# Side work beside a matmul stream: steps weighted by their work, none beside the rotations, and three shared PSUM banks instead of two and one

## The chip, the cores and the metric

The kernel runs on one core of one Trainium2 chip. TensorE (PE) multiplies matrices and writes its products to PSUM; VectorE (DVE) and ScalarE (ACT) read them from there. Each engine works through its own list of instructions in order and waits, where it must, on semaphores. The metric is the device time of one execution in microseconds (us).

## The reference, cut to what matters

One block with two branches on the same normalized input h (512 positions by 2048 channels), both cut from one wide projection:

```
h = rmsnorm(x, g_norm) * (1 + scl) + shift
r_q, r_k, r_v, r_g, n_q, n_kc, ..., m_a, m_b = split(h @ w_in)
y_ret = retention(rope(r_q), rope(r_k), r_v) * silu(r_g)      # 8 heads, chunks of 128
y_nsa = nsa_attention(rope(n_q), ...) * silu(n_g)             # 8 query heads, 2 kv groups
merged = sigmoid(m_a) * (y_ret @ w_up_ret) + sigmoid(m_b) * (y_nsa @ w_up_nsa)
out = rmsnorm(x + gate * (merged @ w_out), g_final)
```

`nsa_attention` is the part that the change schedules: each query attends to compressed keys, to selected blocks and to a window; with 512 positions the last two are causal softmax attentions over all earlier keys, each with its own keys and values. The three outputs are added with gates.

## The kernel before, in words

The projections are the main stream. A weight item of 128x1024 is loaded by SP into one of five raw buffers, ACT rounds it to `whi` (line 267), DVE writes the rest to `wlo` (line 268), and three matmuls (high by high, high by low, low by high) stand for one fp32 product (line 420). A `Group` is one block of 512 output columns: 8 items, 192 matmuls, four accumulators (tiles `g5_0` to `g5_3`) in four large banks. The groups that matter here, in order: g4 (`nq1`), g5 (`rq0`), g6 (`rk0`), g7 (`rv0`), g8 (`rg0`), g9 (`rq1`), g10 (`rk1`), g11 (`rv1`), g12 (`rg1`), g13 and g14 (`ng0`, `ng1`), then eight gate groups.

`Group.block` issues the work of one item as four steps, one accumulator (6 matmuls) each; its first act is to split the weights two items ahead. The last block of a group has two items, so 12 matmuls a step, and each of its steps ends with the evacuation of its accumulator (`self.ev`). For nq, rq and rk this is `rope`: two copies on ACT (lines 496 and 497), three passes on DVE (lines 498 to 500), through one `rot` buffer, so that one rotation follows the other.

After each step `tick` adds `rate` times the items of the step to a credit, and takes steps off the queue `side` while there is credit of 1 (line 383). From g5 on the queue holds `nsa_units`: 16 quads (four heads of one kv group, one 128-row block i of queries, one of the two softmax branches), each with four `scores` (one fp32 matmul of 128*(i+1) columns; mask and minimum on DVE, line 679; exponential on ACT, line 681; reciprocal and scaling on DVE, lines 682 and 683), `turn`s (four transposes into one bank, then a cast on ACT, line 731, and a subtraction on DVE, line 732) and `av`s (three matmuls, line 744). `c_scores`, `c_turn` and `c_av` do the compressed branch. When they are done, `ret_units` (retention) follow at a rate of 0.2; the last part of a head, `r3`, is a chain of some twenty small DVE instructions. What is left of `side` after mb3 is run at once.

PSUM has eight banks: four for groups, one for `o`, two for score tiles (`sbank`) and one for transposed tiles (`tbank`). A tile's bank comes free when the last engine has read the tile.

Tile names in what follows: `sc103` is the score tile of quad 10, head 3; `tp100` the transposes of quad 10, key block 0; `tp30c` those of the compressed branch.

Of the kernel before, what the change touches and what calls it, by code (L numbers as in the profile page):

```python
# [22 lines left out]
NK = D // P  # L23
# [62 lines left out]
def block_kernel(ctx: ExitStack, tc: tile.TileContext, t_in, out):  # L86
# [12 lines left out]
    def bank(tag, bufs, name):  # L99
        return ps.tile([P, 512], F32, tag=tag, bufs=bufs, name=name)  # L100
# [2 lines left out]
        return bank("pg", 4, name)  # L103

    def sbank(name):
        return bank("pss", 2, name)

    def tbank(name):
        return bank("pst", 1, name)

    def obank(name):
        return bank("pso", 1, name)
# [263 lines left out]


    side = deque()
    credit = [0.0]
    RATE_N, RATE_R = 0.72, 0.2  # L380
    rate = [0.0]

    def tick(w=1):
        credit[0] = min(credit[0] + rate[0] * w, 2.0)
        while credit[0] >= 1.0 and side:
            side.popleft()()
            credit[0] -= 1.0

    def flush():
        while side:  # L390
# [2 lines left out]
    class Group:  # L393


        def __init__(self, kind, banks, a_hi, a_lo, nk, ev, k0=0):
            self.kind, self.banks, self.a_hi, self.a_lo, self.nk, self.ev = kind, banks, a_hi, a_lo, nk, ev
            self.kk, self.k0 = 0, k0

        def steps(self, items):  # L400

# [27 lines left out]
        def block(self, items):  # L429
            load(items[0])  # L430
            n0 = w_ord[items[0]]
            split(max(n0 + 2, n0 + len(items) - 1))
            for st in self.steps(items):
                st()
                tick(len(items))

    def run_group(grp, idx, n, between=None, tail=2):

# [18 lines left out]
    hhi = lambda kk: h_hi[kk // 8][:, kk % 8, :]  # L457
    hlo = lambda kk: h_lo[kk // 8][:, kk % 8, :]
# [201 lines left out]
    def nsa_units():  # L660


        quads = [(i, g, br) for i in range(NT) for g in range(2) for br in range(2)]
# [3 lines left out]
        def scores(q, r):  # L667
            i, g, br = quads[q]
            if "pq" not in res:
                res["pq"] = bigt("pq")  # L670
            b = sbank(f"sc{q}{r}")
            n = P * (i + 1)
            h = 4 * g + r
            nc.tensor.matmul(b[:, :n], res["qT"][:, h, i * P:(i + 1) * P], res["kT"][:, 2 * br + g, :n],  # L674
                             start=True, stop=True)
            p = res["pq"][:, count[0] % 8, :]
            count[0] += 1
            sm = wk.tile([P, 3], F32, tag="sm", bufs=3, name=f"sm{q}{r}")
            nc.vector.tensor_tensor_reduce(p[:, :n], b[:, :n], mask[:, 512 - n:], -SCALE, 3.0e38,  # L679
                                           OP.add, OP.min, sm[:, 0:1])  # L680
            nc.scalar.activation(p[:, :n], p[:, :n], AF.Exp, bias=sm[:, 0:1], scale=-1.0, accum_out=sm[:, 1:2])  # L681
            nc.vector.reciprocal(sm[:, 2:3], sm[:, 1:2])
            nc.vector.tensor_scalar(p[:, :n], p[:, :n], sm[:, 2:3], gates[:, i, 3 * h + 1 + br:3 * h + 2 + br],
                                    op0=OP.mult, op1=OP.mult)
            st[q, r] = p

        def c_scores(i, g):
            b = sbank(f"sc{i}{g}c")
            bv = b[:, :P].rearrange("p (r n) -> p r n", r=4)
            for r in range(4):  # L690
                nc.tensor.matmul(bv[:, r, :], res["qT"][:, 4 * g + r, i * P:(i + 1) * P], res["kcT"][:, g, :],
                                 start=r == 0, stop=r == 3, skip_group_check=True)
            p = wk.tile([P, 4, 32], F32, tag="pc", bufs=1, name=f"pc{i}{g}")
            mx = wk.tile([P, 4], F32, tag="mx", bufs=2, name=f"mx{i}{g}")
            nc.vector.tensor_tensor(p, bv, cmask[:, i, None, :].to_broadcast([P, 4, 32]), op=OP.add)
            nc.vector.tensor_reduce(mx, p, axis=AX.X, op=OP.max)
            nc.vector.tensor_tensor(p, p, mx[:, :, None].to_broadcast([P, 4, 32]), op=OP.subtract)
            nc.scalar.activation(p, p, AF.Exp, scale=SCALE)
            sm = wk.tile([P, 4], F32, tag="smc", bufs=2, name=f"smc{i}{g}")
            nc.vector.tensor_reduce(sm, p, axis=AX.X, op=OP.add)  # L700
            nc.vector.reciprocal(sm, sm)
            gt = gate0[:, 4 * g:4 * g + 4] if i == 0 else gates[:, i, 12 * g:12 * g + 12:3]
            nc.vector.tensor_tensor(sm, sm, gt, op=OP.mult)
            nc.vector.tensor_tensor(p, p, sm[:, :, None].to_broadcast([P, 4, 32]), op=OP.mult)
            st["c"] = p
# [17 lines left out]
        def turn(q, m):  # L723
            i, g, br = quads[q]
            b = tbank(f"tp{q}{m}")
            for r in range(4):
                nc.tensor.transpose(b[:, r * P:(r + 1) * P], st[q, r][:, m * P:(m + 1) * P], ident)  # L727
            hi = wk.tile([P, 512], F32R, tag="pT", bufs=3, name=f"pT{q}{m}")
            lo = res["lo"][:, st.get("n", 0) % 2, :]
            st["n"] = st.get("n", 0) + 1  # L730
            nc.scalar.copy(hi, b)
            nc.vector.tensor_tensor(lo, b, hi.bitcast(F32), op=OP.subtract)
            st[q, "T", m] = hi, lo

        def av(q, m):
            i, g, br = quads[q]
            hi, lo = st.pop((q, "T", m))
            if br == 0 and m == 0:
                st["o"] = obank(f"o{q}")
            o = st["o"]  # L740
            c = slice(256 * br + P * g, 256 * br + P * g + P)
            vh, vl = res["v"][:, m, c], res["vl"][m][:, c]
            for n, (l, r) in enumerate(((vh, hi), (vl, hi), (vh, lo))):
                nc.tensor.matmul(o, l, r, start=br == 0 and m == 0 and n == 0, stop=br == 1 and m == i and n == 2,  # L744
                                 skip_group_check=True)
            if br == 1 and m == i:
                if "oT" not in res:
                    res["oT"] = bigt("oT")
                nc.scalar.copy(res["oT"][:, 4 * g:4 * g + 4, i * P:(i + 1) * P], o.rearrange("p (r t) -> p r t", r=4))

        seq = [lambda: scores(0, 0), lambda: scores(0, 1)]
        for q in range(len(quads) + 1):
            last = q == len(quads)
            if not last:
                seq += [lambda q=q: scores(q, 2), lambda q=q: scores(q, 3)]
            if q:
                n = quads[q - 1][0] + 1
                seq += [lambda q=q, m=m: av(q - 1, m) for m in range(max(n - 2, 0), n)]
            if last:
                break  # L760
            i, g, br = quads[q]
            if br == 1:
                seq.append(lambda i=i, g=g: c_turn(i, g))
            seq.append(lambda q=q: turn(q, 0))
            if br == 1:
                seq.append(lambda i=i, g=g: c_av(i, g))
            else:
                seq.append(lambda i=i, g=g: c_scores(i, g))
            nxt = [lambda q=q, r=r: scores(q + 1, r) for r in range(2)] if q + 1 < len(quads) else []
            seq += nxt[:1]  # L770
            for m in range(1, i + 1):
                seq.append(lambda q=q, m=m: turn(q, m))
                if m <= i - 1:
                    seq.append(lambda q=q, m=m: av(q, m - 1))
                if m == 1:
                    seq += nxt[1:]
            if i == 0:
                seq += nxt[1:]
# [156 lines left out]
    idx = 0  # L935
# [46 lines left out]
    i = 0  # L982
# [9 lines left out]
    comp = lambda i, it: comp_slice(i, it[1], it[2])  # L992
    for g in range(2, NG):
        name, kind, _ = GROUPS[g]
        bk = [gbank(f"g{g}_{t}") for t in range(4)]
        idx = run_group(Group(kind, bk, hhi, hlo, NK, evac_in(g)), idx, 8, comp)
        if name == "nq0":
            side.extend(comp_finish())
            rate[0] = 0.25
        if name == "nq1":  # L1000
            flush()
            side.extend(nsa_units())
            rate[0] = RATE_N
        if name == "rg1":
            side.append(lambda: (res.update(nsa_done=True), free.update(raw=free["raw"] + 1)))
            side.append(lambda: rate.__setitem__(0, RATE_R))
            side.extend(ret_units())
        if name == "ng1":
            y_lo["n"] = bigt("ylo_n", F32R)
            for h in range(NH):  # L1010
                nc.gpsimd.dma_start(y_lo["n"][:, h, :], yl_d[1, h])
# [37 lines left out]
    for j in range(4):  # L1049
# [4 lines left out]
        for w in (1, 0):  # L1054
            bk = [gbank(f"u{j}{w}_{t}") for t in range(4)]
# [7 lines left out]
            idx = run_group(grp, idx, 4, gate_item)  # L1063
# [50 lines left out]
    for j in range(4):  # L1114
# [6 lines left out]
        if j == 0:  # L1121
            items = list(range(idx, idx + 8))
# [90 lines left out]
```

## Time and profile before

| | us |
|---|---|
| median of 3 runs (lowest, highest) | 1622.55 (1620.81, 1624.44) |
| the profiled execution's own time | 1619.56 |
| its span, first to last instruction | 1617.8 |
| PE busy | 1577.8 (98%) |
| DVE busy | 738.5 (46%) |
| ACT busy | 493.5 (31%) |
| mean granted TensorE clock, share of full | 0.993 |
| a weight item's load, issue to landing (median) | 3.7 |

The profile is of one execution. A busy PE is a row of matmuls whose ends are modelled, so a matmul's row is longer than the distance to the next one's start; distances between starts say how fast PE goes. A wait is put down to the instruction whose semaphore came last.

### The profile page before, as it was taken

What the parts mean: (1) busy time and instruction counts of PE and PEld (TensorE: products, weight loads), DVE (VectorE), ACT (ScalarE), POOL (GpSimd) and SP (SyncE); (2) the same over time, 40 slices, a digit from 0 to 9 for tenths busy, and PEclk for the clock granted to TensorE, in tenths of its full rate; (3) what the DMA queues carried; (4) which work ended last, traced back from release to release, by engine and by line L of the source; (5) the groups of instructions that cost most, each with busy time, mean ns of one, the idle gap of its engine ahead of it and who ended that gap; (6) DMA issues with size and microseconds to landing.
All of it is one profiled execution on the core that took longest, in us unless ns stands there. A gap on an engine that the chain in (4) does not pass through costs nothing.

```text
span 1617.8 us, 18389 instructions
## 1 busy us (share of the span) xinstructions
PE 1577.8 (98%) x7294; PEld 1254.4 (78%) x7294; DVE 738.5 (46%) x1278; ACT 493.5 (31%) x715; POOL 33.9 (2%) x68
## 2 busy tenths in 40 slices
PE   7999999999999999899999999999999999999997
PEld 2566777877887877678888888888888888878886
DVE  5454534355645446543244343332212566754444
ACT  1232223234433533332233333332222222222223
POOL 2000000000000000000001000000001000010000
PEclk9999999999999999999999999999999999999999
DMA  9885444323233323223534554433335777884322
GB/s 374 332 319 208 135 164 148 93 68 102 67 103 104 96 69 98 92 66 118 185 129 132 193 159 159 130 124 114 108 111 175 262 235 244 261 299 181 104 79 104
DMA packets 88214, 252.50 MB, mean 156 GB/s; under 512 B 9248, under 2 KB 18528, under 8 KB 86976
## 3 DMA queue, kind: packets, MB, share of 16 engines
q1 hardware_dynamic: 80048, 235.71, 43.2%
q0 software_dynamic: 7504, 13.53, 2.7%
q10 hardware_dynamic: 576, 2.10, 0.3%
q8 instruction: 57, 0.93, 0.2%
q14 instruction: 29, 0.24, 0.0%
HBM read 224.03 MB, written 27.26 MB: 155 GB/s over the span
## 4 chain that ended last, share of the span: by engine, by line
PE 89%; DVE 5%; ACT 3%; DMA 2%; issue 1%; SPq 0%; ACTq 0%; DVEq 0%
PE g L420 56%; PE o L420 11%; PE u L420 9%; PE g L922 2%; PE sc L674 2%; PE pa L330 2%; PE o L744 1%; PE tp L727 1%; PE ssq L278 1%; PE phid L613 1%; DMA raw<-in_w_ada 1%; DVE wlo L268 1%; PE ro L841 0%; PE rsc L814 0%; DMA raw<-in_w_un 0%
## 5 line engine op out<-in xcount | busy, mean ns | idle before, releaser
L268 DVE TENSOR_TENSOR wlo<-raw,whi 128x1024 fp32r<-128x1024 f32 x246 | 297.9, 1223 | 470.2 <-ACT whi L267 462.4
L420 PE MATMUL g<-hhi,whi 128*128 128x512 f32 x1088 | 440.8, 405 | 0.0
L420 PE MATMUL g<-hhi,wlo 128*128 128x512 f32 x1088 | 425.9, 391 | 1.1 <-DVE wlo L268 1.1
L420 PE MATMUL g<-hlo,whi 128*128 128x512 f32 x1088 | 425.1, 391 | 0.0
L267 ACT CAST whi<-raw 128x1024 fp32r<-128x1024 f32 x246 | 254.8, 1048 | 474.7 <-PE g L420 220.5
L420 PEld LDWEIGHTS g<-hhi,whi 128*128 128x128 f32 x1088 | 205.2, 189 | 54.9 <-issue 12.1
L420 PEld LDWEIGHTS g<-hhi,wlo 128*128 128x128 f32 x1088 | 204.8, 188 | 45.6 <-DVE wlo L268 1.5
L420 PEld LDWEIGHTS g<-hlo,whi 128*128 128x128 f32 x1088 | 205.2, 189 | 41.8 <-issue 1.9
L420 PE MATMUL g<-whi,hhi 128*128 128x512 f32 x320 | 135.7, 424 | 0.0
L420 PE MATMUL g<-wlo,hhi 128*128 128x512 f32 x320 | 125.8, 393 | 1.0 <-DVE wlo L268 1.0
L420 PE MATMUL g<-whi,hlo 128*128 128x512 f32 x320 | 126.0, 394 | 0.0
L420 PE MATMUL o<-whi,mhi 128*128 128x512 f32 x240 | 95.0, 396 | 0.0
L420 PE MATMUL o<-whi,mlo 128*128 128x512 f32 x240 | 93.4, 389 | 0.0
L420 PE MATMUL o<-wlo,mhi 128*128 128x512 f32 x240 | 93.4, 389 | 0.0
L681 ACT ACTIVATE pq<-pq,sm 128x128 f32<-128x128 f32 (+3 forms) x64 | 36.0, 563 | 137.9 <-DVE sm L679 137.8
L420 PEld LDWEIGHTS g<-wlo,hhi 128*128 128x128 f32 x320 | 60.8, 190 | 15.6 <-issue 1.7
L420 PEld LDWEIGHTS g<-whi,hhi 128*128 128x128 f32 x320 | 60.7, 190 | 15.5 <-issue 2.0
L420 PEld LDWEIGHTS g<-whi,hlo 128*128 128x128 f32 x320 | 60.5, 189 | 13.4
L420 PEld LDWEIGHTS o<-wlo,mhi 128*128 128x128 f32 x240 | 45.1, 188 | 10.3 <-issue 1.0
L420 PEld LDWEIGHTS o<-whi,mhi 128*128 128x128 f32 x240 | 45.1, 188 | 10.1 <-issue 1.0
L420 PEld LDWEIGHTS o<-whi,mlo 128*128 128x128 f32 x240 | 45.1, 188 | 9.4
L674 PE MATMUL sc<-kT,qT 128*128 128x128 f32 (+3 forms) x128 | 45.6, 438 | 4.7 <-DVE sm L679 4.7
(318 smaller groups left out, 1674.8 us busy)
## 6 DMA issues: line engine op xcount, KB each, us to landing
raw<-in_w_in SPq DMA_DIRECT2D x176, 512.0 KB, 3.7
raw<-in_w_ada SPq DMA_DIRECT2D x32, 512.0 KB, 7.8
raw<-in_w_ada SPq DMA_DIRECT2D x16, 1024.0 KB, 8.7
raw<-in_w_gate SPq DMA_DIRECT2D x32, 512.0 KB, 4.7
raw<-in_w_o SPq DMA_DIRECT2D x32, 512.0 KB, 4.1
raw<-in_w_c SPq DMA_DIRECT2D x16, 512.0 KB, 3.8
raw<-in_w_un SPq DMA_DIRECT2D x16, 512.0 KB, 4.6
sg<-ma_d SPq DMA_DIRECT2D x32, 256.0 KB, 3.8
```

The lines of the kernel that those rows point to most:

```text
L267: nc.scalar.copy(hi, r)
L268: nc.vector.tensor_tensor(lo, r, hi.bitcast(F32), op=OP.subtract)
L278: nc.tensor.matmul(ssq, ones, sq, start=kk == 0, stop=kk == NK - 1)
L330: nc.tensor.matmul(pa[j][32 * u:32 * u + 32, :], sc32[:, 4 * b + u, :], rs[u // 2][:, u % 2, :], start=b == 0, stop=b == 3)
L420: nc.tensor.matmul(self.banks[t], l, r, start=kk == 0 and n == 0, stop=kk == self.nk - 1 and n == 2)
L613: nc.tensor.matmul(hid[64 * v:64 * v + 64, :], wins[v, s][:, i, :], craw[v][:, i, :], start=s == 0 and i == 0, stop=s == 7 and i == 3)
L674: nc.tensor.matmul(b[:, :n], res["qT"][:, h, i * P:(i + 1) * P], res["kT"][:, 2 * br + g, :n], start=True, stop=True)
L681: nc.scalar.activation(p[:, :n], p[:, :n], AF.Exp, bias=sm[:, 0:1], scale=-1.0, accum_out=sm[:, 1:2])
L727: nc.tensor.transpose(b[:, r * P:(r + 1) * P], st[q, r][:, m * P:(m + 1) * P], ident)
L744: nc.tensor.matmul(o, l, r, start=br == 0 and m == 0 and n == 0, stop=br == 1 and m == i and n == 2, skip_group_check=True)
L922: nc.tensor.matmul(b, l, r, start=u == 0 and m == 0, stop=u == 3 and m == 2)
```

## The change

It does four things. `tbank` becomes another name for `sbank`, with three banks for both kinds of tile; each new tile takes the bank that has been free longest. Every NSA step has a cost that is taken from the credit instead of 1: 1.6 for scores, 1.2 for a turn, 0.7 for an av, 2.0 for the compressed scores, and the rate rises from 0.72 to 0.95. Two empty steps of cost 2.0 stand ahead of the first scores. And in groups that end with a rotation (rq, rk; not nq), the last block doesn't call `tick`.

```
     def sbank(name):
-        return bank("pss", 2, name)
-
-    def tbank(name):
-        return bank("pst", 1, name)
+        return bank("pss", 3, name)
+
+    tbank = sbank
...
-    RATE_N, RATE_R = 0.72, 0.2
+    RATE_N, RATE_R = 0.95, 0.2
...
         while credit[0] >= 1.0 and side:
-            side.popleft()()
-            credit[0] -= 1.0
+            f = side.popleft()
+            f()
+            credit[0] -= cost.get(f, 1.0)
...
                 st()
-                tick(len(items))
+                if not (self.rot and self.kk == self.nk):
+                    tick(len(items))
...
-        seq = [lambda: scores(0, 0), lambda: scores(0, 1)]
+        seq = [w(2.0, lambda n=n: None) for n in range(2)]
+        seq += [w(1.6, lambda: scores(0, 0)), w(1.6, lambda: scores(0, 1))]
...
-                    seq.append(lambda q=q, m=m: av(q, m - 1))
+                    seq.append(w(0.7, lambda q=q, m=m: av(q, m - 1)))
...
-        idx = run_group(Group(kind, bk, hhi, hlo, NK, evac_in(g)), idx, 8, comp)
+        idx = run_group(Group(kind, bk, hhi, hlo, NK, evac_in(g), rot=name[:2] in ("rq", "rk")), idx, 8, comp)
```

The lines of the file shift by one to two up to `nsa_units` (420 becomes 421, 679 becomes 681) and by eight behind it.

DVE at the start of g5, where the attention begins. Before, from the last pass of nq1's last rotation on:

```order
L500 TENSOR_TENSOR qT_1527<-qT_1527,rotq7_2142 128x512
L268 TENSOR_TENSOR wlo121_2155<-raw121_1992,whi121_2154 128x1024
L268 TENSOR_TENSOR wlo122_2159<-raw122_2032,whi122_2158 128x1024
L679 ISA pq_2168,sm00_2171<-sc00_2169,c_mask_97 128x128
L679 ISA sm00_2171 128x1
L682 RECIPROCAL sm00_2171<-sm00_2171 128x1
```

Now, from the split of the weights on:

```order
L267 TENSOR_TENSOR wlo121_2155<-raw121_1992,whi121_2154 128x1024
L267 TENSOR_TENSOR wlo122_2159<-raw122_2032,whi122_2158 128x1024
L267 TENSOR_TENSOR wlo123_2191<-raw123_2062,whi123_2190 128x1024
L681 ISA pq_2200,sm00_2203<-sc00_2201,c_mask_97 128x128
L681 ISA sm00_2203 128x1
L684 RECIPROCAL sm00_2203<-sm00_2203 128x1
```

The first scores now come behind a third split, that of the next block: on PE they stand after five steps of g5 instead of one.

DVE at the end of g9 (rq1, a rotation) and the start of g10. Before, the rotations of heads 2 and 3 with the steps between them:

```order
L500 TENSOR_TENSOR rq12_4229<-rq12_4229,rotrq12_4230 128x512
L732 TENSOR_TENSOR pTlo_1209<-tp112_4237,pT112_4242 128x512
L498 TENSOR_TENSOR rq13_4257<-g9_3_3849,cosT_186 128x512
L499 TENSOR_TENSOR rotrq13_4258<-rotrq13_4258,sinT_187 128x512
L500 TENSOR_TENSOR rq13_4257<-rq13_4257,rotrq13_4258 128x512
L679 ISA pq_2168,sm122_4267<-sc122_4265,c_mask_97 128x512
L679 ISA sm122_4267 128x1
L682 RECIPROCAL sm122_4267<-sm122_4267 128x1
L683 TENSOR_SCALAR pq_2168<-pq_2168,sm122_4267,gates_184 128x512
L268 TENSOR_TENSOR wlo161_4279<-raw161_4062,whi161_4278 128x1024
```

Now:

```order
L502 TENSOR_TENSOR rq13_4114<-rq13_4114,rotrq13_4115 128x512
L267 TENSOR_TENSOR wlo161_4129<-raw161_3943,whi161_4128 128x1024
L267 TENSOR_TENSOR wlo162_4133<-raw162_3991,whi162_4132 128x1024
L681 ISA pq_2200,sm103_4144<-sc103_4142,c_mask_97 128x384
L681 ISA sm103_4144 128x1
L684 RECIPROCAL sm103_4144<-sm103_4144 128x1
L685 TENSOR_SCALAR pq_2200<-pq_2200,sm103_4144,gates_184 128x384
L734 TENSOR_TENSOR pTlo_1209<-tp100_4174,pT100_4179 128x512
```

The rotations follow each other without a step between them; the fourth score of quad 10 stands behind the rotations and the splits, and the first transposes of that quad (`tp100`, which read it) right behind it. The queue has fallen back by almost two quads here (quad 12 before, quad 10 now).

PE at a compressed turn (quad 13). Before, with six matmuls of one step between the two:

```order
L712 MATMUL tp30c_4559<-ident_113,pc30_4357 32x128 x4
L420 MATMUL g10_3_4275<-hhi1_180,whi165_4438 128x512
L420 MATMUL g10_3_4275<-hlo1_182,whi165_4438 128x512
L420 MATMUL g10_3_4275<-hhi1_180,wlo165_4439 128x512
...
L727 MATMUL tp130_4574<-ident_113,pq_2168 128x128 x4
```

Now:

```order
L714 MATMUL tp30c_4877<-ident_113,pc30_4669 32x128 x4
L729 MATMUL tp130_4886<-ident_113,pq_2200 128x128 x4
```

The two turns wrote one bank in succession before; now they stand side by side and write two different ones.

## Rows read from the trace of the kernel before

**Rows 1.** Who PE waited for, whole span: total us, times, longest.

```profile
PE sc L674 <- DVE sm L679: 4.7, 2, 2.6
PE tp L727 <- DVE pTlo L732: 3.9, 1, 3.9
...
PE tp L727 <- ACT pT01c L716: 0.8, 1, 0.8
...
PE tp L727 <- DVE pq L683: 0.7, 1, 0.7
...
PE tp L727 <- ACT pT11c L716: 0.6, 1, 0.6
```

**Rows 2.** The same view: the main stream's matmuls.

```profile
PE g L420 <- DVE wlo L268: 2.1, 2, 1.1
```

**Rows 3.** Stretches: us, busy us of each engine, then PEclk, DMA share, GB/s.

```profile
330.00:334.00 4.00, 4.00 (x14) 3.20 (x13) 2.66 (x9) 1.62 (x6) 0.00 (x0) 0.60 0.00 1
...
385.00:388.60 3.60, 3.60 (x12) 2.88 (x11) 3.02 (x6) 1.91 (x3) 0.00 (x0) 0.61 0.90 249
388.60:612.00 223.40, 221.22 (x1017) 178.46 (x1016) 114.11 (x250) 88.84 (x163) 0.00 (x0) 1.00 0.28 89
...
684.00:689.00 5.00, 5.00 (x14) 3.78 (x14) 1.92 (x2) 1.63 (x2) 0.00 (x0) 0.58 0.35 120
```

**Rows 4.** Timeline of PE around the first wait (g5): start, us, instruction, [idle before].

```profile
325.37 0.40 PE L420 MATMUL g<-hhi,wlo 128*128 128x512 f32 x1
328.39 0.49 PE L674 MATMUL sc<-kT,qT 128*128 128x128 f32 x2 [2.63 <-DVE sm L679]
```

**Rows 5.** Timeline of ACT, the rotations at the end of g4.

```profile
311.89 0.58 ACT L496 COPY rotq<-g 64x512 f32<-64x512 f32 x1 [1.94 <-PE g L420]
...
315.22 0.58 ACT L496 COPY rotq<-g 64x512 f32<-64x512 f32 x1 [2.16 <-DVE qT L500]
...
322.64 0.58 ACT L496 COPY rotq<-g 64x512 f32<-64x512 f32 x1 [2.16 <-DVE qT L500]
```

**Rows 6.** Timeline of DVE, the end of those rotations and the first scores.

```profile
325.78 2.35 DVE L268 TENSOR_TENSOR wlo<-raw,whi 128x1024 fp32r<-128x1024 f32 x2
328.05 0.28 DVE L679 CUSTOM_DVE_ANT_0 pq<-sc,c_mask 128x128 f32<-128x128 f32 x1
...
329.36 0.28 DVE L679 CUSTOM_DVE_ANT_0 pq<-sc,c_mask 128x128 f32<-128x128 f32 x1
```

**Rows 7.** Timeline of DVE, one score's chain at 256, 384 and 512 columns.

```profile
399.44 0.43 DVE L679 CUSTOM_DVE_ANT_0 pq<-sc,c_mask 128x256 f32<-128x256 f32 x1
...
400.75 0.41 DVE L683 TENSOR_SCALAR pq<-pq,sm,gates 128x256 f32<-128x256 f32 x1
...
519.31 0.56 DVE L679 CUSTOM_DVE_ANT_0 pq<-sc,c_mask 128x384 f32<-128x384 f32 x1 [3.10 <-PE sc L674]
...
520.86 0.48 DVE L683 TENSOR_SCALAR pq<-pq,sm,gates 128x384 f32<-128x384 f32 x1
...
598.58 0.69 DVE L679 CUSTOM_DVE_ANT_0 pq<-sc,c_mask 128x512 f32<-128x512 f32 x1 [2.20 <-PE sc L674]
...
600.36 0.55 DVE L683 TENSOR_SCALAR pq<-pq,sm,gates 128x512 f32<-128x512 f32 x1
```

**Rows 8.** Timeline of PE: a score, a step, transposes, an av, a step.

```profile
511.20 0.81 PE L674 MATMUL sc<-kT,qT 128*128 128x384 f32 x2
511.55 0.69 PE L420 MATMUL g<-whi,hhi 128*128 128x512 f32 x1
...
513.23 0.60 PE L727 MATMUL tp<-ident,pq 128*128 128x128 f32 x4
...
515.06 0.39 PE L744 MATMUL o<-pT,vt 128*128 128x512 f32 x1
...
515.75 0.39 PE L420 MATMUL g<-whi,hhi 128*128 128x512 f32 x1
```

**Rows 9.** Timeline of DVE at the start of g14, behind retention's r3.

```profile
835.05 0.29 DVE L851 BATCH_NORM_STATS2 bst<-ro 128x6 f32<-128x128 f32 x1
...
839.98 2.35 DVE L268 TENSOR_TENSOR wlo<-raw,whi 128x1024 fp32r<-128x1024 f32 x2
```

**Rows 10.** Groups of ACT instructions, 318 to 760 us.

```profile
L565 ACT ACT_TABLE_LOAD x2 | 2.6, 1283 | 0.0
```

More of the change, by code (lines that the diff above doesn't have):

```diff
@@ L378, in block_kernel @@
     side = deque()
+    cost = {}
     credit = [0.0]
-    RATE_N, RATE_R = 0.72, 0.2
+    RATE_N, RATE_R = 0.95, 0.2
     rate = [0.0]
@@ L393, in block_kernel, with __init__ @@
     class Group:
-        def __init__(self, kind, banks, a_hi, a_lo, nk, ev, k0=0):
+        def __init__(self, kind, banks, a_hi, a_lo, nk, ev, k0=0, rot=False):
             self.kind, self.banks, self.a_hi, self.a_lo, self.nk, self.ev = kind, banks, a_hi, a_lo, nk, ev
-            self.kk, self.k0 = 0, k0
+            self.kk, self.k0, self.rot = 0, k0, rot
         def steps(self, items):
@@ L749, in av, with w @@
                 nc.scalar.copy(res["oT"][:, 4 * g:4 * g + 4, i * P:(i + 1) * P], o.rearrange("p (r t) -> p r t", r=4))
-        seq = [lambda: scores(0, 0), lambda: scores(0, 1)]
+        def w(c, f):
+            cost[f] = c
+            return f
+        seq = [w(2.0, lambda n=n: None) for n in range(2)]
+        seq += [w(1.6, lambda: scores(0, 0)), w(1.6, lambda: scores(0, 1))]
         for q in range(len(quads) + 1):
@@ L754, in nsa_units @@
             if not last:
-                seq += [lambda q=q: scores(q, 2), lambda q=q: scores(q, 3)]
+                seq += [w(1.6, lambda q=q: scores(q, 2)), w(1.6, lambda q=q: scores(q, 3))]
             if q:
                 n = quads[q - 1][0] + 1
-                seq += [lambda q=q, m=m: av(q - 1, m) for m in range(max(n - 2, 0), n)]
+                seq += [w(0.7, lambda q=q, m=m: av(q - 1, m)) for m in range(max(n - 2, 0), n)]
             if last:
@@ L763, in nsa_units @@
                 seq.append(lambda i=i, g=g: c_turn(i, g))
-            seq.append(lambda q=q: turn(q, 0))
+            seq.append(w(1.2, lambda q=q: turn(q, 0)))
             if br == 1:
@@ L767, in nsa_units @@
             else:
-                seq.append(lambda i=i, g=g: c_scores(i, g))
-            nxt = [lambda q=q, r=r: scores(q + 1, r) for r in range(2)] if q + 1 < len(quads) else []
+                seq.append(w(2.0, lambda i=i, g=g: c_scores(i, g)))
+            nxt = [w(1.6, lambda q=q, r=r: scores(q + 1, r)) for r in range(2)] if q + 1 < len(quads) else []
             seq += nxt[:1]
             for m in range(1, i + 1):
-                seq.append(lambda q=q, m=m: turn(q, m))
+                seq.append(w(1.2, lambda q=q, m=m: turn(q, m)))
                 if m <= i - 1:
-                    seq.append(lambda q=q, m=m: av(q, m - 1))
+                    seq.append(w(0.7, lambda q=q, m=m: av(q, m - 1)))
                 if m == 1:
```

## The prediction

> **What bounds the kernel now.** I read the busy table first, then the list of what PE waited for, then the stretches with the granted clock, then the timelines of PE, DVE and ACT around each wait. PE is busy in 98% of the span, so only what stops or slows PE can be won. The reader is to see in the list of waits that, behind the start-up, nearly every wait of PE lies in the attention steps: two of scores on DVE, 4.7 us in all, one of transposes on DVE, 3.9, five of transposes on ACT of 0.6 to 0.8 (0.8, 0.8, 0.6, 0.6, 0.6; the first and the last stand in the group), and one of 0.7 on a score's scaling [rows 1]. That is nine waits and 12.7 us. Distances between starts say a little more: in the first case a matmul starts at 325.37 and the next at 328.39, 3.02 us later, where plain ones follow each other by 0.23 (0.69 for the three of an av) [rows 4, 8]. The lost time is thus 2.8 where the list says 2.6, because a matmul's row outlasts the start of the next by 0.17. With nine times 0.17 the waits cost 14.2 us.
>
> The stretches show a second loss. After the waits at 328, 384 and 683 us the granted clock is 0.60, 0.61 and 0.58 for 4.0, 3.6 and 5.0 us; from 388.6 to 612, with three of the short waits in it, it is 1.00 [rows 3]. PE was busy in these three stretches throughout, so the work in them would have taken 4.0*0.40 + 3.6*0.39 + 5.0*0.42 = 5.1 us less at full clock. A wait of 2.1 us and more of idle time was followed by the lower level (1.2 GHz for part of the stretch), waits of up to 0.8 were not.
>
> So the attention steps lose 14.2 + 5.1 = 19.3 us. One more wait is the second of the 2.1 us on the low halves [rows 2]: at 841 us PE waits 1.1 (1.3 by starts) for a split that begins on DVE at 839.98, right behind r3 of retention's first head, which runs there from 835.05 on [rows 9]. Together 20.6 us, and this is all that the change can reach.
>
> **The change part by part.** No matmul is added or removed, so PE's work is the same; only waits move. All times below count from T0, the first matmul of the group behind a rotation.
>
> The backlog at T0 comes first, because each further number hangs on it. Rotations follow each other by 3.33 us (311.89 to 315.22) when nothing stands between them [rows 5]. From the fourth one's first copy (322.64) to the moment at which DVE begins a score behind the two splits (328.05) there are 5.4 us [rows 5, 6]. The first copy starts when step 0 of the last block ends, 3*12*0.23 = 8.3 us ahead of T0 now that no step stands between, plus the 0.2 by which a row outlasts. DVE is then free for the new group's attention steps at -8.1 + 3*3.33 + 5.4 = T0 + 7.3, say 7.4. The first of the two splits is ready at 6.2; PE needs it in the third matmul of the next item, at 4*1.38 plus the steps beside it plus 0.5, which is 6.2 to 8. Nothing is lost there by a margin of a few tenths; it is the tightest cover of this change.
>
> Empty steps ahead of the first scores (g5): sc00 goes to T0 + 6.9 and the fourth score, the first to need a used bank, to T0 + 14. DVE has read sc00 by 9. The wait of 2.8 us and its slow clock (1.6) go; tp00 then comes one step behind sc03 and may wait for its scaling. I take 0.2 (0 to 0.5).
>
> Three banks: the five waits for ACT are cases in which `tp..c` and the next turn write one bank; two casts and a subtraction must end between them. Now the turn gets another bank, last read some 4 us earlier, and all five go (3.4 + 5*0.17 = 4.3 us). The wait at 683 is the same bank between tp132 and tp133, behind a rotation; with no step beside rotations and three banks it goes too (4.1, and 2.1 of clock), and so does the one at 384 (2.3, and 1.4). Start-up tiles in the common banks: beside the long-lived `pa` the products of group k alternate over two banks as before, so 0.
>
> No steps beside rotations: what is late next is the first turn after T0, whose last transpose needs the quad's fourth score, which now stands on DVE behind the whole backlog. Behind a waiting turn on PE stands the main stream, so each such wait counts in full. There are four places.
> - g6 (128 columns): DVE does sc20 and sc21 at 1.31 each [rows 6], a split whose cast stands behind two exponentials on ACT, sc22 and sc23, and is done at 14.6. PE reaches the last transpose of tp20 at 14.4. I take 0.2.
> - g7 (256 columns): three scores of 1.72 [rows 7] end at 12.5. PE: seven steps of 1.38, three scores of about 0.45 with their slower following step, an av, three transposes: 12.0. I take 0.6.
> - g10 (384 columns): one score of 2.03 [rows 7], ready at 7.4 + 2.0 + 0.1 = 9.5. PE: 1.38 + 0.35 + 1.68 + 0.69 + 1.38 + 0.69 + 1.38 [rows 8] = 7.55, and three transposes make it 7.9. A wait of 1.6 to 1.8; I take 1.7. Its idle time lies between the waits that left the clock alone and those that didn't, so half of 1.7 for the clock: 0.9 (0 to 1.7).
> - g11 (512 columns): three chains of 2.33 [rows 7], a subtraction and a split end at 17; PE arrives at 19. Nothing.
>
> Weights and rate: the queue ends in g13, eight steps after where g13 starts, instead of in g12. Nobody waits for it: the gates that need all of attention are evacuated in g13's last block. ACT switches tables more often at the end of rg1, five loads of 1.28 [rows 10] where one stood, 5.1 us more on ACT within some 14 us of PE. ACT falls back by about 1 us there, and its next cast is due 5 us later: 0, and 1 if it is due earlier than I think.
>
> Retention moves back by some 12 steps, with its loads. SP's first loads of `rt` now wait up to 3 us for the last av; the weight loads behind them are five items of 5.4 us ahead, so 0. The stores on POOL's queue move with it and are read back after mb3, groups later: 0. The chain at 841 is gone, since r3 of head 0 falls into g14's second block: 1.3 won. But r3 of head 1 now falls between the evacuations of ng1's last block, where every evacuation needs ACT and DVE in turn and r3 holds both. I count 16.1 us for that chain up to the first split of g15 and 16.9 until PE needs it. I take 0.4 (0 to 1.5).
>
> Sum against the profiled execution: 1619.56 - 20.6 + (0.2 + 0.2 + 0.6 + 1.7 + 0.9 + 0 + 0.4) = 1603.0. The median of the runs lies 3.0 above the profiled execution, so the forecast for the median is 1606. With all new waits at nothing it is 1602; with 0.5, 1, 1.5, 1.8 and 1.7, and 1.5 at ng1, 8.0 us, it is 1610. That is the likeliest case's own range.
>
> **Clock.** The row first: from 388.6 to 612 us PE had three waits of 0.6 to 0.8 between its bursts and the granted clock stayed 1.00 [rows 3]. The Trainium skill, TensorE: Matmul & The Clock Gate, section "A second HAM failure mode: psum-queue depth-cycling", says that where PE's products cycle through banks, short idles between groups of matmuls are enough for the clock to swing between its levels. By that rule, each of the four waits that I leave would bring a slow stretch of 1.7, 6.8 in all instead of 0.9, and the forecast would be 1612. This trace disagrees for waits up to 0.8.
>
> **The rivals.**
> - Waits for data take the place of waits for banks, and are larger than I count. If DVE is 1.5 us later at each T0 than I have it, the four first turns wait 1.5 more each, and three or four of them are long enough for the slow clock (1.7 each, less the 0.9 counted): 6 + 5 to 6 us, and the time is 1617. For it: DVE is the engine behind all the large waits. Against: the backlog is read from four undisturbed rotations.
> - The clock swings after every short wait, the case above: 1612. For it only the lower level after long waits; against it the stretch at 1.00.
> - The change doesn't do what it says: the backlog of rotations and splits is the same work in the same order, and each wait only moves to the next instruction that needs DVE. Then the time is within 3 us of before. Against it: the first scores and the turns behind a compressed turn wait for a bank alone, and that is now free.
> - Slower: the rotations, with PE going ahead without pauses, take longer than 3.33 each. The place is the first low half after each T0, with a margin of 0.2 at g6. If the distance grows by x, DVE is 3x later, and PE waits about 3x, plus 1.7 of clock, at each of four starts. The 16 us that I forecast are used up at 4*(3x + 1.7) = 16.3, x = 0.8, and above x = 1.1 the kernel is slower than before by more than 3 us; at 1.5 it would be 1631. In the profile nothing stretches an undisturbed rotation.
>
> **How the numbers follow.** Forecast 0.68 (1602 to 1610), larger data waits 0.15 (1611 to 1618), swinging clock 0.08 (1612), no effect 0.04, slower 0.05. A difference of 0.2%, 3.2 us, is what can be told from no change. Faster is 0.68 + 0.15 + 0.08 = 0.91, the same 0.04, slower 0.05. The range goes from 1601, the forecast with nothing new and a little of luck, to 1615, which takes in the clock case and half of the larger waits.
>
> **What would show it.** Right: no wait of PE on score or transpose banks between 321 and 790 us; waits for a score's scaling at tp100 of about 1.7, at tp40 of about 0.6, and none on low halves; a granted clock of 1.00 but for some us behind tp100; no wait at g14's second item. Wrong: a wait on `wlo` right after a rotation group, transposes that still wait for the cast of the one before, rotations at more than 3.4, or a wait at g15 behind ng1.

## The result, and the profile after

The changed kernel takes 1602.7 us (median; 1600.93 to 1603.81) where the kernel before, beside it, took 1622.92: a ratio of 0.9875, with an interval of 0.9858 to 0.9892. It is 20.2 us faster. The profiled execution took 1602.33 us, 17.2 less than that of before (1619.56).

Who PE waited for in the changed kernel, whole span (engine, line, what it waited for: total us, times, longest):

```profile
PE ssq L277 <- DVE sq L276: 7.9, 1, 7.9
PE pa L329 <- DMA raw<-in_w_ada: 4.4, 5, 1.9
PE g L421 <- DVE wlo L267: 2.5, 2, 1.4
PE tp L729 <- DVE pq L685: 1.9, 2, 1.5
```

The row on scores, with its two waits, and the seven rows on transposes ([rows 1] shows four of the seven) have become one row with two waits, 1.9 in all. No wait for a bank is left, neither on DVE's reading of a score (`sm`) nor on ACT's cast of a compressed turn. The main stream's row [rows 2] has two waits again, 2.5 for 2.1, but one of them is a new one, below.

Stretches of the changed kernel (us, busy us of each engine, granted clock, DMA share, GB/s):

```profile
330.00:380.00 50.00, 50.00 (x239) 41.34 (x238) 27.33 (x66) 19.40 (x39) 0.00 (x0) 1.00 0.28 93
...
440.00:595.00 155.00, 154.47 (x708) 125.12 (x706) 75.91 (x159) 61.29 (x106) 0.00 (x0) 1.00 0.29 91
596.57:600.57 4.00, 4.00 (x23) 3.40 (x22) 2.91 (x6) 1.61 (x3) 0.00 (x0) 1.00 0.49 146
600.57:760.00 159.43, 159.43 (x713) 125.35 (x712) 80.10 (x154) 61.98 (x101) 0.00 (x0) 1.00 0.26 86
```

PE is busy in nearly all of each stretch and the clock is 1.00 in every one, where [rows 3] had 0.60, 0.61 and 0.58. The stretch at 596.57 lies right behind the longest wait that is left in the attention.

That wait stands at the start of g10. Timeline of DVE there, the two splits behind the last rotation and the fourth score:

```profile
591.63 2.35 DVE L267 TENSOR_TENSOR wlo<-raw,whi 128x1024 fp32r<-128x1024 f32 x2
593.90 0.55 DVE L681 CUSTOM_DVE_ANT_0 pq<-sc,c_mask 128x384 f32<-128x384 f32 x1
...
595.44 0.48 DVE L685 TENSOR_SCALAR pq<-pq,sm,gates 128x384 f32<-128x384 f32 x1
```

and PE (the first row is g10's first matmul):

```profile
586.45 0.39 PE L421 MATMUL g<-hhi,whi 128*128 128x512 f32 x1
...
593.98 0.49 PE L729 MATMUL tp<-ident,pq 128*128 128x128 f32 x3
595.97 0.33 PE L729 MATMUL tp<-ident,pq 128*128 128x128 f32 x1 [1.50 <-DVE pq L685]
```

DVE begins the score at 593.90, 7.45 after g10's first matmul. PE reaches `tp100` at 593.98, 7.53 after it, does three transposes and waits for the fourth score's scaling until 595.97. The other wait on that row is `tp40`, 0.36 of idle time at 432.64.

The rotations at the end of g9, on ACT:

```profile
578.49 0.58 ACT L498 COPY rotrq<-g 64x512 f32<-64x512 f32 x1 [1.84 <-PE g L421]
...
581.83 0.59 ACT L498 COPY rotrq<-g 64x512 f32<-64x512 f32 x1 [2.16 <-DVE rq L502]
```

They follow each other by 3.34 us, as the undisturbed ones of [rows 5] do by 3.33.

The new wait of the main stream stands at the start of g15, 871.88. It is not where [rows 9] had one: that chain is gone. DVE and then POOL around it:

```profile
860.52 0.69 DVE L866 TENSOR_TENSOR ro<-ro,rt 128x512 f32<-128x512 f32 x1
...
865.91 0.69 DVE L539 TENSOR_TENSOR ng<-ng,oT 128x512 f32<-128x512 f32 x1 [0.73 <-ACT ng L538]
870.00 0.69 DVE L543 TENSOR_TENSOR yln<-ng,yhi_n 128x512 fp32r<-128x512 f32 x1 [3.40 <-DMA yl_d<-yln]
870.61 2.35 DVE L267 TENSOR_TENSOR wlo<-raw,whi 128x1024 fp32r<-128x1024 f32 x2
```

```profile
863.49 0.53 POOL L544 DMA_DIRECT2D yl_d<-yln  x1 [6.39 <-DVE yln L543]
```

The last evacuation of ng1 (870.00) waits 3.4 us for a store: its tile is one of four `ev` buffers, and the store of the tile that had this buffer last was issued at 863.49. Of the eight stores of `yln` one took 6.4 us, where the median is 2.3:

```profile
DMA to landing us min/median/max: 2.3/2.3/6.4
```

What else was under way is on SP's queue:

```profile
861.28 0.33 SPq L799 DMA_DIRECT2D rt<-rq_d  x1
...
863.15 0.50 SPq L805 DMA_DIRECT2D dm<-in_dm  x1
863.75 11.30 SPq L236 DMA_DIRECT2D raw<-in_w_in  x4
```

The moment r3 of head 1 has read its `rt` tile for the last time (860.52 on DVE), head 3's five loads go out, four of 256 KB into that buffer and one of 64 KB, and a weight item of 512 KB behind them. The last row above takes four weight items together; looked at in a window of its own, it is one item at 863.75, and the next goes out only after the store has landed:

```profile
871.85 0.33 SPq L236 DMA_DIRECT2D raw<-in_w_in  x1
```

E8 and e10 below test whether these transfers are the reason.

### The profile page after: what moved, and what is told of

Same layout as the page of the kernel before. It is cut to its first block, busy times and chain, and to the rows that moved or that the text cites. A ratio compares the mean times of both kernels' runs of the same rounds, so it can differ in the third digit from the quotient of the medians.

```text
span 1600.3 us, 18392 instructions
## 1 busy us (share of the span) xinstructions
PE 1570.2 (98%) x7294; PEld 1250.6 (78%) x7294; DVE 739.1 (46%) x1278; ACT 502.5 (31%) x721; POOL 33.9 (2%) x68
## 4 chain that ended last, share of the span: by engine, by line
issue 54%; PE 41%; DMA 2%; DVE 2%; ACT 1%; POOL 0%; DVEq 0%; POOLq 0%; ACTq 0%
PE g L421 21%; PE o L421 11%; PE u L421 8%; DMA c_mask<-in_mask 1%; DMA raw<-in_w_ur 1%; DVE wlo L267 1%; DMA yl_d<-yln 0%; DVE mtmp L1048 0%; DVE sg L1047 0%; PE ro L849 0%; ACT mhi L1051 0%; PE rsc L822 0%; PE ro L852 0%; PE rkv L835 0%; PE pgate L1088 0%
## 5 line engine op out<-in xcount | busy, mean ns | idle before, releaser
L421 PE MATMUL u<-yhi_n,wlo 128*128 128x512 f32 x128 | 50.0, 391 | 0.1
```

What stands on the lines that cost most here:

```text
L421: nc.tensor.matmul(self.banks[t], l, r, start=kk == 0 and n == 0, stop=kk == self.nk - 1 and n == 2)
```

## The experiments

The median of each kernel stands beside that of the kernel before, run on the same chip, and the ratio with its interval of 95%. The ratio is taken over all runs, so it is not exactly that of the two medians.

| | kernel | us | before | ratio |
|---|---|---|---|---|
| e1 | before + three banks | 1612.31 | 1621.38 | 0.9943 (0.9928 to 0.9958) |
| e2 | before + no steps beside rotations | 1609.69 | 1621.38 | 0.9929 (0.9915 to 0.9944) |
| e3 | before + weights, rate, empty steps | 1631.34 | 1621.38 | 1.0056 (1.0037 to 1.0075) |
| e11 | e1 and e2 together | 1608.27 | 1622.42 | 0.9917 (0.9897 to 0.9938) |
| e4 | changed - three banks | 1613.53 | 1621.38 | 0.9958 (0.9946 to 0.9971) |
| e5 | changed + steps beside rotations | 1612.14 | 1621.94 | 0.9942 (0.9927 to 0.9957) |
| e6 | changed - empty steps | 1605.14 | 1621.94 | 0.9905 (0.9888 to 0.9921) |
| e7 | changed, again | 1604.33 | 1621.58 | 0.9897 (0.9881 to 0.9914) |
| e8 | changed, head loads 5 steps later | 1602.18 | 1621.58 | 0.9884 (0.987 to 0.9899) |
| e10 | changed, head loads 10 steps later | 1602.64 | 1621.25 | 0.9893 (0.9877 to 0.991) |
| e9 | changed + hold behind rotations | 1600.55 | 1621.58 | 0.9871 (0.9857 to 0.9886) |

**E1, the banks alone.**

```
-        return bank("pss", 2, name)
-    def tbank(name):
-        return bank("pst", 1, name)
+        return bank("pss", 3, name)
+    tbank = sbank
```

> The kernel before with three shared banks alone. Theory (each part takes away its own waits, and some waits turn from banks to data): the five waits of turns behind a compressed turn go (4.3 us); at 328 us sc02 finds a third bank (2.8 and 1.6 of clock go), but the first transposes then wait about 1.5 for sc03's scaling; behind the rotations half of the waits at 384 and 683 stays, since the same data stand behind the same rotations on DVE; the wait at 841 stays. About 1612 (1608 to 1616). Rival (a wait for a bank moves whole to the next instruction that needs DVE): within 3 us of 1622.9 less the 4.3, 1616 to 1621.

```profile
PE tp L726 <- DVE pq L682: 5.2, 5, 2.7
```

9.1 us faster, as the theory had it, and no wait for a bank is left. But two terms of the theory were wrong, and their errors cancel. At the start of g5 I expected a wait of 1.5; there are three, of 0.34, 0.99 and 2.66, and the granted clock behind them is 0.50 and 0.55 for 4 us each, some 3.8 us more. Of the waits at 384 and 683 half was expected to stay; both are gone. The other two of the five are 0.5 in g6 and the 0.7 at g10, which the kernel before has too (at 623 us). So the banks alone make the start of g5 slower than it was, and win elsewhere.

**E2, no steps beside the rotations, alone.**

```
                 st()
-                tick(len(items))
+                if not (self.rot and self.kk == self.nk):
+                    tick(len(items))
```

> The kernel before without steps beside the rotations of rq and rk, and nothing else. Theory: the waits at 384 (2.3 and 1.4 of clock) and 683 (4.1 and 2.1) go; the one at the first scores stays (2.8 and 1.6), three or four of the turns behind a compressed turn still wait 0.8 (those with one step between), new ones of 1 to 1.3 for scores in g7 and g11: about 1613 (1609 to 1618). Rival (the rotations are the same work and the wait only comes later): 1620 to 1623.

```profile
PE sc L675 <- DVE sm L680: 2.6, 1, 2.6
PE tp L728 <- DVE pq L684: 1.8, 2, 1.6
PE tp L728 <- ACT pT21c L717: 0.6, 1, 0.6
```

11.7 us faster. Rows like the last there are four. The wait of `sc02` for a bank and those of turns behind compressed turns stay; no score or turn waits long behind a rotation (the 1.6 is new and stands at the first quad; the new waits of 1 to 1.3 in g7 and g11 that I expected did not come). The wait of `sc02` is as long as before, but no lower clock followed it in this profile (last section). The wait at 841 is gone as well: with fewer steps retention comes later (r3 of its first head begins at 840.4 instead of 835.1, though the main stream is ahead). A wait of 0.5 at g15 stands in its place.

**E3, weights, rate and empty steps alone.** The changed kernel with `tbank` and `sbank` as before and without `rot=`. (Not every step has a weight of its own: the compressed turn and its av keep a cost of 1.)

> The kernel before with the weights, the rate of 0.95 and the two empty steps, but with two banks and one, and with steps beside the rotations. Theory: eight compressed turns now stand closer to the next turn; five with one step between wait 0.85 each, three with none between 2.2 each and 1.7 for the clock; behind the rotations 5 to 7 more; in all about 1627, slower than before (1620 to 1632). Rival (the parts act each by itself, and the weights bring their share of the 20 us): 1613 to 1618.

```profile
PE tp L730 <- ACT pT30c L719: 4.5, 1, 4.5
PE tp L730 <- ACT pT21c L719: 4.2, 1, 4.2
PE tp L730 <- DVE pq L686: 3.5, 1, 3.5
```

Slower than before by 0.56%. The two longest waits are turns that stand right behind a compressed turn in the last block of a rotation group. ACT there:

```profile
606.90 0.58 ACT L499 COPY rotrq<-g 64x512 f32<-64x512 f32 x1 [2.98 <-PE g L422]
607.50 0.58 ACT L500 COPY rotrq<-g 64x512 f32<-64x512 f32 x1
608.10 0.57 ACT L717 CAST pT21c<-tp21c 32x512 fp32r<-32x512 f32 x1
610.87 0.57 ACT L719 CAST pT21c<-tp21c 32x512 fp32r<-32x512 f32 x1 [2.20 <-DVE pT21c L718]
```

The second cast waits 2.2 us for DVE, which has the rotation's three passes to do between the two. PE, with one transpose bank, stands until the cast is done: 4.24 us of idle time before 611.50. So the part that packs the steps closer is a loss by itself; e4 and e5 below put one of the other two parts beside it.

**E11, banks and rotations together**, without weights, empty steps and the higher rate.

> The kernel before with three shared banks and no steps beside the rotations; no weights, no empty steps, the rate of 0.72. Theory: the two together take the waits of turns behind compressed turns and those behind rotations; what stays is the start of g5, where the first transposes come 3.5 steps earlier than in the changed kernel and wait for the scores' scaling as with the banks alone (4.0 and 2.2 of clock), about 1.3 at tp120, which stands five steps behind a rotation, and about 1 at g15, since r3 of head 1 falls into the last block of ng1: 1608 (1605 to 1610), 13 to 14 faster than before. Rival (the two overlap, and the weights bring what is left): 1611 to 1613, no better than the better of the two alone.

```profile
PE tp L727 <- DVE pq L683: 4.2, 4, 2.7
```

1608.27 for 1608. The wait at `tp120` did not come. What is left is the start of g5, with three of the four waits and the longest of them, 2.66, and a wait of 0.5 at g15. Behind that start the granted clock is 0.51 and 0.63 for 4 us each, some 3.4 us more (2.2 expected). In the whole change these waits and this clock are gone. What the weights, the rate and the empty steps add is the distance from 1608.27 to the 1602.7 and 1604.33 of the whole change, 4 to 6 us, or 3 to 6 when each is taken against the kernel before on its own chip (14.2 less for e11, 20.2 and 17.2 for the whole change).

**E4, the changed kernel with two banks and one.**

> The changed kernel with two score banks and one transpose bank. Theory: the waits of turns behind a compressed turn come back, five of 0.85 and two (quads 13 and 15, which now stand side by side) of 2.2 with 1.7 of clock, and the scores behind each rotation wait for a bank that DVE reads behind the backlog, 4 and 1.7 of clock at sc42, 1 at sc22: about 1620 (1612 to 1625). Rival (the banks are worth the waits of before, 4.3): 1607.

```profile
PE tp L730 <- ACT pT30c L719: 2.0, 1, 2.0
PE tp L730 <- ACT pT31c L719: 2.0, 1, 2.0
...
PE sc L677 <- DVE sm L682: 1.4, 1, 1.4
...
PE tp L730 <- ACT pT21c L719: 0.6, 1, 0.6
```

The two turns side by side wait 2.0 each and five others 0.6, as expected. Of the waits of scores for a bank only one came, 1.4 in g7, where I expected 4 and in g6 another 1: DVE reads the first score of a pair ahead of the rotations, so that only the second holds its bank through the backlog. The median is 1613.53 where I expected 1620 and the rival 1607, 6.5 off on either side: the waits that the rival left out came, the large one that I added did not.

**E5, the changed kernel with steps beside the rotations.** Without `rot=name[:2] in ("rq", "rk")`.

> The changed kernel with steps beside the rotations again. Theory: the waits at tp40 (0.5) and tp100 (1.7) go, since their scores stand further ahead; tp20, which now stands three steps behind the rotations, waits about 4 and costs 2 of clock, tp50 about 1, others 0 to 1: 1607 (1603 to 1612). Rival (a rotation doesn't care for steps beside it): 1600 to 1601.

```profile
PE tp L729 <- DVE pq L685: 3.4, 1, 3.4
PE g L421 <- DVE wlo L267: 2.9, 3, 1.1
PE o L722 <- ACT pT30c L718: 1.3, 1, 1.3
```

`tp20` waits 3.4 (4 expected), and the waits at `tp40` and `tp100` go, as expected. New to me: with three banks the wait behind a compressed turn moves to its av (`o`, line 722), which needs the same delayed cast, 1.3 in quad 13 and 1.0 in quad 11; and a wait of 0.76 on the first low halves behind the rotation at g7 and the wait of [rows 9], 1.10, are in the row on `wlo`. The median, 1612.14, lies just above my range. Rotations with a score step beside each, on ACT:

```profile
367.88 0.58 ACT L498 COPY rotrq<-g 64x512 f32<-64x512 f32 x1
...
371.87 0.58 ACT L498 COPY rotrq<-g 64x512 f32<-64x512 f32 x1
```

3.99 us apart instead of 3.33: a score step beside a rotation costs the chain 0.66.

With e5 and e4 each pair of parts has been run. Each against the kernel before on its own chip: the weights, rate and empty steps cost 10.0 alone (e3); beside the banks they change little (e5 is 9.8 faster than before, e1 9.1); beside the bare rotations they cost 3.8 (e4 7.9 faster, e2 11.7); only beside both they win 3 to 6.

**E6, the changed kernel without the empty steps.** `seq = []` in place of the two.

> The changed kernel without the two empty steps. Theory: with a third bank the scores wait little (sc03 needs the bank of sc00, read 7.9 us behind the start of g5, PE is there at 8.3); but the first transposes need the fourth score's scaling, which DVE ends some 12.6 behind the start, and PE is there at about 10: a wait of 2 to 3 with 1.7 of clock, 1606 to 1607; all later steps stand four steps earlier, which moves the waits at tp40 and tp100 by an amount that I can't say (0 to 2 either way). Rival (the empty steps are needed for the banks): a wait of sc03 of over 1. Rival (they do nothing): 1602.7.

```profile
PE tp L729 <- DVE pq L685: 4.6, 5, 2.7
```

The first transposes wait 2.67 us and the lower clock follows, as expected (0.60 in the next 4 us), and no score waits for a bank. The four steps by which the rest moved forward took away the waits at `tp40`, `tp100` and g15 and brought 0.5 and 1.0 at `tp20`. 1605.14 against 1604.33 (e7) and 1602.7: what the empty steps are worth by themselves can't be told from this.

**E7, e8 and e9, on one chip**, the changed kernel again, with later head loads, and with a hold.

> The changed kernel as it is, beside the next two on one chip: 1602.7, waits of 0.5 at tp40, 1.7 at tp100 and 1.6 on wlo at the start of g15.

It came to 1604.33, 17.2 us less than the kernel before beside it, with waits of 0.35 (idle) at `tp40`, 1.50 at `tp100` and 0.95 on `wlo` at g15. The store of `yln` took 5.9 us here, and DVE waited 2.9 for it. The edit of e8:

```
             def a(h=h):
-                if 0 < h + 1 < RH and h > 0:
-                    load(h + 1)
...
             def b(h=h):
+                if 0 < h + 1 < RH and h > 0:
+                    load(h + 1)
```

> The changed kernel with a head's loads for retention issued five steps later (in r1's step instead of r0's), so that the loads of head 3 don't stand on SP ahead of four weight items in the last block of ng1. r3 of head 1 stays where it is. Theory (the last evacuation waits for a buffer whose store lands 6.4 us late beside those transfers): the store lands in under 3 us, DVE doesn't wait for it, the split starts 2.7 us earlier, and the wait of 1.6 at g15 shrinks to 0 to 0.3; 1601.2. Rival (as in the prediction: r3 itself takes DVE from the chain of evacuations): the wait stays 1.6.

The result is between: the store landed in 5.0 us instead of 6.4 (5.9 in e7), DVE waited 1.95 for it instead of 3.40 (2.9), the wait of PE at g15 is gone, and r3 stands where it stood. That is against the rival. But "under 3 us" was missed, since head 3's loads still went out at 861.44, the moment r3 freed their buffer. What changed is one weight item (the text of e10 says two). It went out ahead of the head's loads, and the next one behind the store:

```profile
853.13 0.33 SPq L236 DMA_DIRECT2D raw<-in_w_in  x1
...
870.56 0.35 SPq L236 DMA_DIRECT2D raw<-in_w_in  x1
```

So the head's loads alone make the store take 5.0. E10 moves them to r2's step, further back on SP, behind a weight item that must wait for a buffer.

> The changed kernel with a head's loads for retention issued ten steps later (in r2's step). With five steps later, the loads of head 3 still started at 861.4, as soon as r3 of head 1 had freed their buffer, but two of the weight items had gone out before them: the store of yln landed in 5.0 instead of 6.4 us, DVE waited 1.95 for it instead of 3.4, and the wait at g15 was gone. Theory (the store is slowed by the transfers that start right ahead of it, head loads and weight items alike): now another weight item, which must wait for a buffer, stands ahead of the head's loads on SP, they start behind 868, the store lands in 2.3 to 3, DVE doesn't wait for it and the split starts near 868; PE doesn't wait at g15; 1601 to 1602 beside 1602.7. Rival (the store is slow for another reason, such as its place in POOL's queue): 5 us and more again.

Stores of `yln`, then SP's queue, in e10:

```profile
DMA to landing us min/median/max: 2.3/2.3/2.3
```

```profile
842.60 29.95 SPq L236 DMA_DIRECT2D raw<-in_w_in  x5
872.65 0.50 SPq L799 DMA_DIRECT2D rt<-rq_d  x1
```

The head's loads start at 872.65, behind the stores; all eight stores take 2.3 us, DVE waits for none, PE has no wait at g15. Nothing of the arithmetic has moved, and the store has its old place in POOL's queue. This shows the cause, the burst of loads beside the store, and what each part of it costs: 2.3 us without it, 5.0 with the head's loads, 5.9 and 6.4 with the weight item too. The DMA share (mean busy share of the 16 DMA engines) was 0.94 to 1.02 from 863.5 to 868 in the changed kernel, and 0.31 to 0.35 beside the same store in e10. What is shown is this wait; in the times it can't be told from the spread. E8's median is 2.2 below e7's, but their runs overlap, and e10, 18.6 below the kernel before on its chip, lies between the 17.2 and 20.2 of the changed kernel.

**E9, a hold behind each rotation group.**

```
-    RATE_N, RATE_R = 0.95, 0.2
+    RATE_N, RATE_R = 0.95, 0.19
...
                 if not (self.rot and self.kk == self.nk):
                     tick(len(items))
+            if self.rot and self.kk == self.nk:
+                credit[0] -= 2.0
```

> The changed kernel with 2.0 taken from the credit at the end of each rotation group, and retention at a rate of 0.19, so that r3 falls into no block at the end or the start of ng0 and ng1. Theory: the first turns behind a rotation come about two steps (2.8 us) later and no longer wait for their fourth score (0.5 and 1.7 gone), and the wait at g15 goes (1.6): 3.8 us faster than the changed kernel, 1599. Rival (DVE's backlog grows with the scores that now all stand behind the rotation, and the first turns still wait): 1601 to 1603.

```profile
PE g L421 <- DVE wlo L267: 1.2, 2, 1.0
PE u L421 <- DVE wlo L267: 0.9, 2, 0.5
```

No score, transpose or av waits, and there is no wait at g15. The 1.0 of the first row is a wait in the start-up, at 179 us, which every kernel here has; its other wait is 0.2 on a low half behind the rotation at g11, the cover that the prediction called the tightest. The second row lies behind 1249 us. 1600.55 against 1604.33 on the same chip, 3.8 less, as expected, and no run of one reaches the runs of the other (1599.12 to 1602.12, and 1603.54 to 1606.62). It has the lowest median here, but against the kernel before its ratio (0.9871) can't be told from that of the changed kernel's first measurement (0.9875). It changes two things, so by itself it doesn't say which of them took the wait at g15 away; its stores all take 2.3 us.

## Why the prediction was right

Forecast 1606 (likeliest case 1602 to 1610, range 1601 to 1615), measured 1602.7.

- What can be reached, 20.6: right. All nine waits of the attention, the lower clock behind three of them and the wait at 841 are gone from the profile of after. The 17.2 between the profiled executions and the 3.8 of new waits make 21.0.
- The backlog, T0 + 7.4: at g10 7.45, by the rows above. This number carried the rest. Its tightest cover, the first low half behind a rotation, held: no wait on `wlo` there.
- `tp100`: PE there at 7.53 behind T0 (7.55 predicted), the wait 1.67 between starts (1.7 predicted). `tp40` 0.53 (0.6). `tp00` and `tp20` nothing (0.2 each). e9 shows them to be what they were said to be: with the same steps two later they are gone.
- Clock, 0.9 for `tp100` (0 to 1.7): 0, the clock is 1.00 behind it, here and in e7, e8 and e10. That also decides against the swinging clock: no wait that is left in the profiles of this kernel brought the lower level.
- The wait at g15, 0.4 (0 to 1.5): the step that failed, and a sign of being wrong that the prediction itself had named. Measured 1.6, just outside its bounds, and not by the way described, r3's instructions between the evacuations. What costs is what r3 sets free: loads on SP that had waited for its buffer and go out from 2.2 us ahead of a store that the last evacuation needs (e8, e10). I counted retention's loads as nothing, since the weight loads behind them were far ahead, and its stores too; the transfer that the loads slow is a third one, the store of `yln`.
- The sum: 0.53 + 1.67 + 1.61 = 3.8 new waits for 4.0. The profiled execution should have taken 1603.0 and took 1602.33. That the sum fits so well is in part luck: 1.3 forecast for the clock, `tp00` and `tp20` did not come, and 1.2 more than forecast came at g15.
- Table loads: five at the end of rg1, as forecast (750.83 to 758.90), and no wait of PE there.
- To the median I added 3.0, since the median of before lay that much above its profiled execution; that of after lies 0.4 above its own. Most of the 3.3 between forecast and measurement is this step. The medians of before on the other chips, 1621.25 to 1622.42, lie 0.1 to 1.3 below the one used.
- The rivals. Larger data waits: none. (With three slow stretches their price was 6 + 4, not 6 + 5: 3 times 1.7 less 0.9 is 4.2.) No effect: e1 and e11 show that waits for a bank do turn into waits for data at the start of g5, where these are longer than the one they replace, but into few and short ones behind the rotations (0.5 in g6 in e1) and none behind the compressed turns. Slower by longer rotations: they stayed at 3.33, with nothing beside them; e5 shows 3.99 where a score step stands beside each. A side of the change that makes the kernel slower did exist and was not among the rivals: the weights, the rate and the empty steps alone cost 10 us (e3).

## What to carry to other kernels

Side work can be packed closer to a matmul stream only when it has the buffers and the free engines for it: the denser schedule alone cost 10 us, two better conditions alone won 9 and 12 and together 14, all three 17 to 20. Behind a burst of serial work on another engine, work out when that engine is free again (here 7.4 us) and place the first consumer just behind that time. And look at what a freed buffer lets loose: a load that has waited for it starts at once, and a store beside it can take nearly three times as long (6.4 us for 2.3).

## What was not expected of the hardware

The clock doesn't follow from the length of one wait. Stretches of 4 us, each 0.6 us behind a wait of PE; first e2, whose first score waits 2.63, the same instruction with the same idle time as in [rows 4]:

```profile
333.03:337.03 4.00, 4.00 (x20) 3.33 (x19) 2.37 (x11) 1.93 (x5) 0.00 (x0) 1.00 0.21 84
```

then e5, behind 3.45 of idle time, and e3 behind 3.45:

```profile
381.04:385.04 4.00, 4.00 (x23) 3.43 (x22) 3.55 (x7) 2.04 (x5) 0.00 (x0) 1.00 0.70 241
```

```profile
382.09:386.09 4.00, 4.00 (x16) 3.45 (x15) 3.56 (x6) 1.83 (x4) 0.00 (x0) 0.61 0.69 240
```

and e4, behind 2.04:

```profile
706.61:710.61 4.00, 4.00 (x14) 3.23 (x12) 0.69 (x1) 0.58 (x1) 0.00 (x0) 0.62 0.00 2
```

Waits of 2.63 and 3.45 left the clock at 1.00 once and were followed by 0.60 and 0.61 another time; of two waits of 2.04 in e4 both were followed by the lower level (0.62 and 0.57), one of the same length in e3 was not. Waits of 1.2 to 1.55 that stood alone (e2 to e5, and the changed kernel, also in e7, e8 and e10) never were, eleven in all. From g5 to g15, over all profiles here, the lower level followed 8 of 11 waits of 2.0 to 3.5 us and each of the three above 3.9. What decides in between stays open, and a forecast can only give such a wait a chance of the lower clock; for a wait as long as that at `tp100` the half that I took was too much. A profile shows one execution, too: over the six of e4 the mean granted clock went from 0.994 to 0.998.
